# Seven inner products for P7 of the output stage, formed in place

## The chip, the cores and the metric

The kernel runs on one core of a Trainium2 chip. The metric is the device time of one execution in microseconds. Before the change it is 910.41 us, the median of three runs (909.86 to 911.19).

## What is computed

One layer of a streaming encoder on 4096 rows of 1024 channels: an RMS norm, a pooling mixer, a residual addition, a final RMS norm. With depth 1 only the pooling mixer runs:

```
def pool_mixer(h, in_w, group_w, group_b, scale, out_w):
    u, gate = jnp.split(h @ in_w, 2, axis=-1)
    ug = u.reshape(b, s, POOL_GROUPS, POOL_GROUP_DIM)
    pooled = jnp.stack([trailing_mean(ug[:, :, g], w) for g, w in enumerate(POOL_WINDOWS)],
                       axis=2) - ug
    mixed = jnp.einsum('bsgc,gcd->bsgd', pooled, group_w) + group_b
    y = mixed.reshape(b, s, POOL_WIDTH) * scale * jax.nn.silu(gate)
    return y @ out_w

h = h + pool_mixer(rms_norm(h, norm_w[0]), ...)
return rms_norm(h, final_norm_w)
```

## The kernel before

Matrices are float32. Each operand of a product is split into a high and a low part (`split`: ACT copies the high part in a shorter format, DVE subtracts it from the operand), and a product takes three passes: high by high, high by low, low by high. The three large products are done by a Strassen scheme of seven products P1 to P7 instead of eight. Stages "a" and "b" make the mixer's two halves in four blocks of 1024 rows and store y to DRAM (`yd`). The stage "o", which the change concerns, multiplies y by the output weights, adds x and applies the final norm, in eight blocks of 512 rows. In the code the blocks count from 0, so that blocks 3 to 8 of the text are b = 2 to 7 (`b > 1`).

In an output block the products run in the order P1, P7, P6, P2, P5, P4, P3. A product covers two banks of PSUM (j = 0, 1), each with four slices of the inner dimension times three passes: 24 matmuls of 128 x 512. `split_o` forms the left operand (for P7 the difference of two quarters of y) and splits it into one of four operand buffers `ops`, taken in turn by `next_op`. `evict_o` moves banks out: P1 is copied by ACT into the banks of "y" as a seed for P6, P5 and P3; P7, P6 and P2 are copied by ACT into the row tiles `hs`, to which GpSimd's accumulating DMAs add x (`add_h`); P5, P4 and P3 are added to the row tiles by DVE. After P4 the upper 256 rows of a block are complete, after P3 the lower ones, and `finish` handles them: ACT squares the two row tiles with a running sum into a junk tile, `inverse` takes the root on ACT, a reciprocal on DVE and five small steps on GpSimd, then DVE scales the two tiles and SP stores them to `out`. The last block loads x into its row tiles beforehand and ends in smaller pieces.

P2 of blocks 3 to 8 is done by a second, inner scheme of seven products (`split_inner`, `product_inner`, `add_inner`). Each inner product is 2 slices x 3 passes = 6 matmuls of 128 x 256. The inner left operand takes two of the operand buffers: the plain quarters and the four sums. The inner weights P1, P2, P3 are quarters of the weights of P2 that lie there split anyway; the four others are formed during block 2 (`load_inner`, `form_inner`) and kept, split, in four tiles.

Working tiles come from two pools: `st` (11 tiles of 128 x 1024) and `vt` (8 tiles). `take` gives the tile that has been free longest, `give` returns it; a tile whose rows are being stored is given back at once, and its next user waits for the store. Loads and splits run ahead of the products by a number of steps, `load_reach` and `split_reach`. The program is recorded in this order and then ordered for each engine by a scheduler, which `tc.issue_after` and `tc.high_priority` steer.

Of the kernel before, what the change touches and what calls it, by code (L numbers as in the profile page):

```python
# [64 lines left out]
def kernel(  # L65
# [55 lines left out]
    def renew(t):  # L121
        i = next(i for i, u in enumerate(sts) if u is t)
        return mem.tile([P, D], F32R, tag=f"st{i}", name=f"inner{i}")
# [514 lines left out]
    def load_inner():  # L638
        inner_w["raw"] = [take() for _ in range(2)]
        for h, u in enumerate(inner_w["raw"]):  # L640
            nc.sync.dma_start(out=u, in_=wod[P2][h])

    def form_inner(stage):

        pattern, sizes = "p (n k s a) -> p n k s a", dict(n=2, k=2, s=2)
        if stage == 0:
            us = inner_w.pop("raw")
            b11, b12 = (quarter(us[0], j) for j in range(2))
            b21, b22 = (quarter(us[1], j) for j in range(2))
            raw = inner_w["sums"] = [take(pattern, **sizes) for _ in range(2)]  # L650
            (t3, t2), (t1, t4) = ([r[:, n] for n in range(2)] for r in raw)
            sub(t3, b22, b12)
            add(t2, t3, b11)
            sub(t1, b22, t2)
            sub(t4, b21, t2)
            for u in us:
                give(u)
            return
        r = inner_w["sums"][stage - 1]
        hi, lo = (kept.pop().rearrange(pattern, **sizes) for _ in range(2))  # L660
        copy(hi, r)
        sub(lo, r, hi.bitcast(F32))
        give(r)
        for n, i in enumerate(((P7, P6), (P5, P4))[stage - 1]):
            inner_w[i] = [v[:, n] for v in (hi, lo)]
        for i, (h, j) in {P1: (0, 0), P2: (1, 0), P3: (1, 1)}.items():
            inner_w[i] = [quarter(w[P2][h][:, s], j) for s in range(2)]

    def split_inner(u):
# [8 lines left out]
        ts = [  # L678
            next_op("p (s g k j c) -> p s g j k c", s=2, g=2, k=2, j=2),
            next_op("p (s n k c) -> p s n k c", s=2, n=4, k=2),  # L680
        ]
        split(ts[0].rearrange("p s g j k c -> p s (g k) (j c)"), u)
        split(ts[1], v)
        give(v)
        t = {P1: ts[0][:, :, 0, 0], P2: ts[0][:, :, 1, 0], P4: ts[0][:, :, 1, 1]}
        t.update({i: ts[1][:, :, n] for n, i in enumerate((P7, P6, P5, P3))})
        return t

    def product_inner(i):

        t, sets = inner["t"], inner["sets"]
# [4 lines left out]
        for k in range(2):  # L696
            a = [t[i][:, s, k] for s in range(2)]
            b = [inner_w[i][s][:, k].rearrange("p s a -> p a s") for s in range(2)]
            ps = bank.rearrange("p (a s) -> p a s", s=2)[:, half * P : (half + 1) * P]
            for n, (x1, x2) in enumerate(((a[0], b[0]), (a[0], b[1]), (a[1], b[0]))):  # L700
                latest[0] = nc.tensor.matmul(  # L701
                    ps, x1, x2, start=i in (P1, P7) and k + n == 0, stop=k == 1 and n == 2,
                    skip_group_check=True,
                ).ins
# [11 lines left out]
    def product_out(i, t, sets, last):  # L716
# [6 lines left out]
        for j in range(2):  # L723
            if j == 1 and inner and i == P5:
# [165 lines left out]
    def load_o(b, i):  # L890
# [7 lines left out]
        elif i == P2:  # L898
            s["12"] = load_y(b, 0, 1)
            load_h(b, 1)  # L900
        elif i == P5:
# [586 lines left out]
```

## Time and profile before

| | us |
|---|---|
| median of 3 runs | 910.41 |
| profiled execution, its own time | 910.49 |
| its span, first to last instruction | 908.7 |
| TensorE busy | 900.7 |
| DVE busy | 715.5 |
| ACT busy | 485.9 |
| GpSimd busy | 84.6 |

How it is read: TensorE is PE in the profile, and PEld its loads of weights, which overlap the matmuls. A block of the output stage from block 3 on takes 35.77 us. The group lines give an engine's line and operation with out<-in, the count, the busy time, the mean ns of one, and the idle time of the engine ahead of them with what ended it. L603 is a matmul of a plain product, L701 one of an inner product, L159 and L156 a subtraction and an addition on DVE, L165 a copy on ACT, L943 a square, L947 the last scaling, L1067 an eviction by addition, L884 the DMAs that add x.

### The profile page before, as it was taken

The page shows a single profiled execution, that of the slowest core. Times are in us where ns is not written, and L with a number is a line of the kernel's source. Part 1 is how long each engine was busy: PE and PEld are TensorE (multiplying, and loading weights), DVE is VectorE, ACT ScalarE, POOL GpSimd, SP SyncE. Part 2 cuts the span into 40 slices and gives each one's busy share as a digit, 9 for nine tenths or more (in the row PEclk, how much of TensorE's full clock was granted, in tenths as well). Part 3 has the DMA queues.
Part 4 walks back from the last instruction along what each step waited for, and adds up shares of the span by engine and source line. Part 5 has one row for each costly group of instructions (what it writes and reads, how often), then busy time and mean ns, then how long its engine had stood idle before and what let it go on. Part 6 is the DMA issues. An engine that isn't in the chain of part 4 may idle for free.

```text
span 908.7 us, 11590 instructions
## 1 busy us (share of the span) xinstructions
PE 900.7 (99%) x4320; PEld 790.1 (87%) x4320; DVE 715.5 (79%) x843; ACT 485.9 (53%) x735; POOL 84.6 (9%) x166
## 2 busy tenths in 40 slices
PE   9999999999999999999999999999999999999997
PEld 7888888888888888888888888888888898988886
DVE  3889995985995997685786599599759768868686
ACT  7869547447446555355345445645545535445444
POOL 0020100100110000000000000001122113212200
PEclk9999999999999999999999999999999999999999
DMA  9987776577575454134616715618585675675732
GB/s 343 401 300 230 268 241 240 190 267 245 218 271 193 162 207 140 47 140 138 255 72 217 267 70 174 200 54 225 179 234 160 169 205 162 163 220 156 180 139 94
DMA packets 70841, 178.10 MB, mean 196 GB/s; under 512 B 6528, under 2 KB 24320, under 8 KB 70784
## 3 DMA queue, kind: packets, MB, share of 16 engines
q1 hardware_dynamic: 58160, 144.82, 46.0%
q0 software_dynamic: 11904, 31.48, 13.3%
q10 hardware_dynamic: 720, 1.06, 0.3%
q8 instruction: 34, 0.56, 0.3%
q14 instruction: 23, 0.19, 0.1%
HBM read 116.50 MB, written 60.83 MB: 195 GB/s over the span
## 4 chain that ended last, share of the span: by engine, by line
PE 95%; DVE 2%; DMA 1%; ACT 1%; issue 0%; DVEq 0%; ACTq 0%; SPq 0%
PE bank L603 89%; PE bank L701 3%; PE bank L406 3%; DMA st<-wvd 1%; DMA t3d<-st 0%; DMA early<-in_group_w 0%; DVE vt L1067 0%; DVE st L159 0%; ACT st L974 0%; ACT st L446 0%; DVE vt L162 0%; PE bank L472 0%; DVE op L159 0%; DVE vt L1026 0%; DVE st L156 0%
## 5 line engine op out<-in xcount | busy, mean ns | idle before, releaser
L603 PE MATMUL bank<-op,w 128*128 128x512 f32 x2688 | 581.2, 379 | 0.2 <-ACT st L165 0.2
L603 PEld LDWEIGHTS bank<-op,w 128*128 128x128 f32 x2688 | 507.8, 189 | 72.9 <-ACT st L165 0.6
L603 PE MATMUL bank<-w,op 128*128 128x512 f32 (+1 forms) x1212 | 262.2, 377 | 0.0
L603 PEld LDWEIGHTS bank<-w,op 128*128 128x128 f32 x1212 | 226.0, 189 | 31.0
L159 DVE TENSOR_TENSOR op<-st,op 128x1024 fp32r<-128x1024 f32 x129 | 156.5, 1220 | 76.4 <-ACT op L165 76.0
L165 ACT ACTIVATE op<-st 128x1024 fp32r<-128x1024 f32 x129 | 134.7, 1052 | 123.3 <-PE bank L603 82.6
L165 ACT ACTIVATE vt<-bank 128x512 f32<-128x512 f32 x105 | 61.4, 593 | 44.7 <-PE bank L603 44.2
L159 DVE TENSOR_TENSOR op<-vt,op 128x1024 fp32r<-128x1024 f32 x43 | 52.4, 1220 | 20.8 <-ACT op L165 20.6
L165 ACT ACTIVATE op<-vt 128x1024 fp32r<-128x1024 f32 x43 | 45.0, 1052 | 28.9 <-PE bank L603 24.9
L165 ACT ACTIVATE st<-bank 128x512 f32<-128x512 f32 x67 | 39.0, 592 | 38.0 <-PE bank L603 26.1
L884 POOL DMA_DIRECT2D st<-in_x x19 | 16.9, 894 | 387.7 <-DVE op L159 354.1
L159 DVE TENSOR_TENSOR st<-st,st 128x1024 f32<-128x1024 f32 (+1 forms) x43 | 46.7, 1108 | 3.2 <-ACT st L943 1.3
L165 ACT ACTIVATE bank<-bank 128x512 f32<-128x512 f32 x48 | 27.9, 581 | 35.6 <-PE bank L603 35.4
L755 DVE TENSOR_TENSOR_SCAN vt<-vt,window 128x1040 f32<-128x1040 f32 x16 | 38.1, 2379 | 2.8 <-ACT vt L165 2.7
L159 DVE TENSOR_TENSOR w<-st,w 128x1024 fp32r<-128x1024 f32 x25 | 30.2, 1220 | 11.7 <-ACT w L165 11.7
L165 ACT ACTIVATE w<-st 128x1024 fp32r<-128x1024 f32 x25 | 26.0, 1052 | 16.3 <-PE bank L603 10.8
L806 DVE SCALAR_TENSOR_TENSOR st<-vt,colt,st 128x512 f32<-128x512 f32 x46 | 32.4, 746 | 1.7 <-ACT st L165 1.6
L165 ACT ACTIVATE st<-st 128x1024 f32<-128x1024 f32 x16 | 16.9, 1058 | 29.9 <-DVE st L156 29.7
L801 DVE SCALAR_TENSOR_TENSOR vt<-vt,vt 128x1024 f32<-128x1024 f32 x24 | 29.3, 1221 | 0.3
L947 DVE SCALAR_TENSOR_TENSOR vt<-vt,ors,st 128x1024 f32<-128x1024 f32 x18 | 22.5, 1282 | 8.0 <-POOL ors L225 8.0
L162 DVE TENSOR_TENSOR st<-st,vt 128x1024 f32<-128x1024 f32 x22 | 26.1, 1216 | 2.1 <-DMA vt<-rd 2.1
L1067 DVE TENSOR_TENSOR st<-bank,st 128x512 f32<-128x512 f32 x23 | 15.8, 689 | 13.8 <-PE bank L603 13.7
(136 smaller groups left out, 661.6 us busy)
## 6 DMA issues: line engine op xcount, KB each, us to landing
st<-in_xt SPq DMA_DIRECT2D x28, 512.0 KB, 5.9
sd<-st POOLq DMA_DIRECT2D x28, 512.0 KB, 4.3
st<-sd SPq DMA_DIRECT2D x24, 512.0 KB, 4.4
yd<-st SPq DMA_DIRECT2D x23, 512.0 KB, 2.6
st<-in_x SPq DMA_DIRECT2D x20, 512.0 KB, 6.3
st<-yd SPq DMA_DIRECT2D x20, 512.0 KB, 4.7
out<-vt SPq DMA_DIRECT2D x18, 512.0 KB, 4.5
st<-wod SPq DMA_DIRECT2D x15, 512.0 KB, 3.4
```

Of the source, the lines that this page charges most:

```text
L159: return nc.vector.tensor_tensor(out=dst, in0=a, in1=b, op=ALU.subtract)
L162: nc.vector.tensor_tensor(out=dst, in0=a, in1=b, op=ALU.mult)
L165: return nc.scalar.activation(dst, src, func)
L406: latest[0] = nc.tensor.matmul(ps, a[:, kk, 2 * j + t, :], maps, start=t + m == 0, stop=t == 1 and m == len(pairs) - 1,).ins
L603: latest[0] = nc.tensor.matmul(ps, a, b, start=start and n == 0, stop=stop and n == 2, skip_group_check=True).ins
L701: latest[0] = nc.tensor.matmul(ps, x1, x2, start=i in (P1, P7) and k + n == 0, stop=k == 1 and n == 2, skip_group_check=True,).ins
L755: nc.vector.tensor_tensor_scan(out=sums_[:, HIST:], data0=flat[:, HIST:], data1=flat[:, HIST - win : 2 * end - win], initial=first_sum, op ...
L801: nc.vector.scalar_tensor_tensor(out=s[:, :, at : at + H], in0=s[:, :, at : at + H], scalar=1.0 / win, in1=v[:, :, HIST:], op0=ALU.mult, o ...
L806: nc.vector.scalar_tensor_tensor(out=sg[:, j], in0=s[:, j, at : at + H], scalar=bias_c[2 * grp + j], in1=sg[:, j], op0=ALU.add, op1=ALU.mult,)
L884: nc.gpsimd.dma_start(out=hs[b][half, j][:, n], in_=x[row_of(b, half, j), n * H : (n + 1) * H], accum_op=ALU.add,)
L947: nc.vector.scalar_tensor_tensor(out=us[j], in0=us[j], scalar=rs[:, j : j + 1], in1=fw[0], op0=ALU.mult, op1=ALU.mult,)
L1067: partial["added"] = nc.vector.tensor_tensor(out=dst, in0=src, in1=dst, op=ALU.add).ins
```

## The change

P7 of blocks 3 to 8 is also done as seven inner products. Unlike P2's, they are not added to row tiles one by one. Two banks make four cells of 128 x 256 (`cell`). `clear_seven` sets two of them to zero on ACT, which writes zeros during P3 of the block before. Inner products are accumulated into the cells, and copies between cells on ACT and two additions on DVE make the sums in place (`product_seven`, parts 0 to 3). Parts 0 and 1 run between the two banks of P1, part 2 in P7's place, part 3 behind P6. P7's banks are evicted there, just before P6's. One inner product (m5) is set aside in a row tile of the block, in the last block in a fresh tile.

For this the left operand of P7 is split by `split_inner` too; its four sums go into two tiles of their own (`own_op`) instead of an operand buffer. The inner weights of P7 and P2 are formed in place in the loaded tiles and split one by one (`sum_inner`, `split_weight`, `forming`), during blocks 2 and 3. Eight tiles of `st` are kept for good instead of four, in the "o" stage of blocks 1 and 2.

`finish` no longer scales and stores; `close` does so one step later. The row tiles of a block, and the load of x into half of them, are taken at P1 and P2 instead of two or more steps ahead. P5's operand is split one step ahead instead of two.

```
+    def clear_seven(b):
+        seven["v"] = sets_of("o", b)["v"]
+        for n in (0, 3):
+            nc.scalar.activation(cell(n), eps.to_broadcast([P, 2 * P]), AF.Copy, scale=0.0)
+
+    def product_seven(part, b):
+        def into(i, n):
+            leaf(seven["t"], inner_w[P7], i, seven["v"][n // 2], n % 2)
+        if part == 0:
+            into(P5, 3)
+            into(P1, 0)
+            if b == NBO - 1:
+                seven["held"] = take()
+                seven["m5"] = seven["held"][:, 0, 0 : 2 * P]
+            else:
+                seven["m5"] = hs[b][1, 0][:, 1, 0 : 2 * P]
+            copy(seven["m5"], cell(3))
+            copy(cell(2), cell(0))
+        elif part == 1:
+            into(P6, 2)
+            into(P2, 0)
+            copy(cell(1), cell(2))
+        elif part == 2:
+            into(P7, 2)
+            into(P3, 1)
+            add(cell(3), cell(2), seven["m5"])
+            add(cell(1), cell(1), seven["m5"])
+            if b == NBO - 1:
+                give(seven.pop("held"))
+        else:
+            into(P4, 2)
...
     def run(n, between=None, behind=None, seeds=4):
         kind, b, i = steps[n]
         sets = sets_of(kind, b)
-        if kind == "o":
+        if kind == "o" and b < NBO - 1 and i in (P1, P2):
+            load_h(b, int(i == P1))
+        if kind == "o" and b > 1 and i == P1:
+            seven["t"] = split_up.pop(n + 1)
+            product_out(i, split_up.pop(n), sets, False, lambda j: product_seven(j, b))
+            evict_o(b, i, sets)
+        elif kind == "o" and b > 1 and i == P7:
+            product_seven(2, b)
+        elif kind == "o" and b > 1 and i == P6:
+            product_out(i, split_up.pop(n), sets, False)
+            product_seven(3, b)
+            evict_o(b, P7, sets)
+            evict_o(b, i, sets)
+        elif kind == "o":
+            if i == P3 and 0 < b < NBO - 1:
+                clear_seven(b + 1)
             product_out(i, split_up.pop(n), sets, n == len(steps) - 1)
             evict_o(b, i, sets)
...
     def finish(b, half):
...
-        rs = inverse(b, half, ss)
+        closing.append((b, half, us, inverse(b, half, ss)))
+
+    def close():
+        b, half, us, rs = closing.pop(0)
         for j in range(2):
             nc.vector.scalar_tensor_tensor(
                 out=us[j], in0=us[j], scalar=rs[:, j : j + 1], in1=fw[0],
...
     def split_inner(u, own=False):
...
+        if own:
+            sums_op = [t.rearrange("p x (y k c) -> p (x y) k c", y=2, k=2) for t in own_op]
+            latest_copy[0] = copy(sums_op[0], v).ins
+            latest_split[0] = sub(sums_op[1], v, sums_op[0].bitcast(F32)).ins
...
     def split_reach(kind, b, i):
-        return 2 if kind == "o" and (b, i) != (0, P1) else 1
+        return 2 if kind == "o" and (b, i) != (0, P1) and not (b > 1 and i == P5) else 1
...
+    forming = {
+        (1, P7): lambda: (load_inner(P7),),
+        (1, P6): lambda: (sum_inner(P7), split_weight(P7, P5)),
+        (1, P2): lambda: (split_weight(P7, P6), split_weight(P7, P7)),
+        (1, P5): lambda: (split_weight(P7, P4), end_weights(P7), load_inner(P2)),
+        (1, P4): lambda: (sum_inner(P2),),
+        (1, P3): lambda: (split_weight(P2, P7), split_weight(P2, P6)),
+        (2, P1): lambda: (split_weight(P2, P5), split_weight(P2, P4), end_weights(P2)),
+    }
...
-        if kind == "o" and b == 1 and len(kept) < 4 and not inner_w:
-            while len(kept) < 4 and len(st.free) > 2:
-                kept.append(st.keep())
-            if len(kept) == 4:
-                load_inner()
-        elif kept:
+        if kind == "o":
+            while len(gathered) < 8 and st.free and len(st.free) + len(vt.free) > 4:
+                gathered.append(st.keep())
+                (kept if len(gathered) not in (3, 4) else own_op).append(gathered[-1])
+        if closing:
+            close()
+        if kind == "o" and b > 0:
             keep[0] = 0
```

More of the change, by code (lines that the diff above doesn't have):

```diff
@@ L636, in quarter @@
         return u.rearrange("p k (s a) -> p k s a", s=2)[:, :, :, j * P : (j + 1) * P]
[L638 to L667, printed above, removed]
@@ new lines, in split_weight, with end_weights, split_inner @@
+    def split_weight(i, p):
+        if p == P5:
+            home = [quarter(w[i][0][:, s], 1) for s in range(2)]
+        else:
+            t = kept.pop().rearrange("p k (h s a) -> p h k s a", h=2, s=2)
+            home = [t[:, s] for s in range(2)]
+        copy(home[0], raws[i][p])
+        sub(home[1], raws[i][p], home[0].bitcast(F32))
+        inner_w[i][p] = home
+    def end_weights(i):
+        for r in raws.pop(i)["held"]:
+            give(r)
+    own_op, gathered = [], []
+    def split_inner(u, own=False):
@@ L695, in product_inner @@
         }.get(i, (sets["spare"][0], 0))
[L696 to L704, printed above, removed]
+        leaf(inner["t"], inner_w[P2], i, bank, half, i in (P1, P7))
     def add_inner(bank, *places):
@@ L723, in product_out @@
         for j in range(2):
+            if between:
+                between(j)
             if j == 1 and inner and i == P5:
@@ L911, in split_o @@
             sub(s["3"], s["11"], s["21"])
+            if b > 1:
+                t = split_inner(s["3"], True)
+                give(s.pop("3"))
+                return t
+        t = next_op("p (s a b) -> p s a b", s=2, a=4)
+        if i == P7:
+            pass
         elif i == P6:
```

71 lines of the change are left out of this document (52 added, 19 removed).

## The prediction

> **What bounds the kernel now.** I read the page's header and busy times first, then who waited for whom on TensorE, then the chain that ended last in the output stage.
>
> ```profile
> span 908.7 us, 11590 instructions
> ...
> PE 900.7 (99%) x4320; PEld 790.1 (87%) x4320; DVE 715.5 (79%) x843; ACT 485.9 (53%) x735; POOL 84.6 (9%) x166
> ```
> ```profile
> PE bank L406 <- DMA early<-in_group_w: 0.4, 1, 0.4
> PE bank L603 <- ACT st L165: 0.2, 1, 0.2
> ```
> ```profile
> 712.80 25.90 PE bank L603 x120
> 738.70 3.35 PE bank L701 x30
> 742.05 2.59 PE bank L603 x12
> 744.64 0.67 PE bank L701 x6
> 745.31 2.59 PE bank L603 x12
> 747.90 0.67 PE bank L701 x6
> 748.57 25.90 PE bank L603 x120
> ```
>
> TensorE is busy for 99% of the span and never waits in the output stage: matmul follows matmul. So whatever shortens TensorE's list shortens the kernel, and every wait put into that list lengthens it one for one. The rows give two prices: 25.90/120 = 0.2158 us for a matmul of 512 columns, and 3.35/30 = 0.1117 us for one of 256. The second is more than half of the first.
>
> The other engines have time to spare on average. These are DVE, then ACT, in block 5's stretch, and TensorE in the last one (columns: stretch, its length, busy time, clock, DMA share, GB/s).
>
> ```profile
> 774.47:810.24 35.77, 25.57 (x34) 1.00 0.67 189
> ```
> ```profile
> 774.47:810.24 35.77, 17.56 (x27) 1.00 0.67 189
> ```
> ```profile
> 881.78:908.70 26.92, 20.32 (x126) 0.98 0.21 79
> ```
>
> TensorE's last matmul ends at 881.78 + 20.32 = 902.1, so 6.6 us of span lie behind it, and 910.49 - 908.7 = 1.8 us around the span.
>
> **What the change takes off TensorE.** P7 of blocks 3 to 8 was 24 matmuls of 512 columns, 24 x 0.2158 = 5.18 us. It becomes 7 x 6 = 42 of 256, 42 x 0.1117 = 4.69 us. That saves 0.49 us a block, 2.93 us in all. Were nothing late, the profiled 910.49 would become 907.56.
>
> **What it puts on the other engines.** The rows of block 5 give the prices: first DVE's, then ACT's.
>
> ```profile
> 787.91 1.21 DVE L159 TENSOR_TENSOR vt<-st,vt 128x1024 f32<-128x1024 f32 x1
> 789.05 0.42 DVE L159 TENSOR_TENSOR st<-st 128x256 f32<-128x256 f32 x1
> 789.50 0.42 DVE L159 TENSOR_TENSOR st<-st,st 128x256 f32<-128x256 f32 x1
> 789.84 0.68 DVE L1067 TENSOR_TENSOR st<-bank,st 128x512 f32<-128x512 f32 x1
> 790.48 1.23 DVE L159 TENSOR_TENSOR op<-vt,op 128x1024 fp32r<-128x1024 f32 x1
> ...
> 792.29 0.16 DVE L210 RECIPROCAL ors<-otmp 128x2 f32<-128x2 f32 x1
> 792.37 0.67 DVE L1067 TENSOR_TENSOR vt<-bank,vt 128x512 f32<-128x512 f32 x1
> 793.67 2.48 DVE L947 SCALAR_TENSOR_TENSOR st<-st,ors,st 128x1024 f32<-128x1024 f32 x2 [0.63 <-POOL ors L225]
> ```
> ```profile
> 783.49 1.06 ACT L165 ACTIVATE op<-st 128x1024 fp32r<-128x1024 f32 x1 [5.36 <-PE bank L603]
> 784.46 1.04 ACT L165 ACTIVATE op<-vt 128x1024 fp32r<-128x1024 f32 x1
> ...
> 798.11 1.06 ACT L943 ACTIVATE st<-vt 128x1024 f32<-128x1024 f32 x1 [2.54 <-DMA out<-st]
> 799.08 0.19 ACT L943 ACTIVATION_READ_ACCUMULATOR st<-vt 128x1 f32 x1
> 799.17 0.58 ACT L165 ACTIVATE bank<-bank 128x512 f32<-128x512 f32 x1
> ...
> 801.70 0.28 ACT L206 ACTIVATE otmp<-oss,eps 128x2 f32<-128x2 f32 x1
> ```
>
> From start to start in a full queue, a DVE operation on 1024 elements costs 1.13 us (1.22 to whoever waits for its result), an eviction of 512 costs 0.60 to 0.64, one of 256 costs 0.34 (0.45 if the next needs it), the two scalings 2.40. From reciprocal to scaling through POOL is 793.67 - 792.29 = 1.38. ACT's copy costs 0.97 (1.06 to its reader), a square 1.06 (1.25 with its sum read), a bank's copy 0.52 to 0.58. The row at 798.11 matters most: ACT waited there for a tile whose rows were still being stored. The scaling began at 793.67, its first half took 1.28, so that store held the tile for 798.11 - 794.95 = 3.1 us. The other prices:
>
> ```profile
> L974 ACT ACTIVATE st<-vt 128x256 f32<-128x256 f32 x2 | 0.8, 409 | 0.0
> ```
> ```profile
> out<-vt SPq DMA_DIRECT2D x16, 512.0 KB, 4.6
> st<-yd SPq DMA_DIRECT2D x10, 512.0 KB, 4.8
> ...
> out<-st SPq DMA_DIRECT2D x5, 512.0 KB, 3.4
> ```
>
> A block gains on DVE four sums of 256 (4 x 0.42), the second split of P7 (1.22) and two additions in the banks (2 x 0.42): 3.7 us. On ACT it gains the copy of that split (1.06) and five pieces of 256 (two clearings, three copies between banks; at most 5 x 0.41 by the row above): 3.1 us. DVE goes from 25.6 to about 29.3 of 35.28 us, ACT to 20.7. Neither is full, so their sums cost nothing. Once, around block 3, P7's inner weights are formed too: two loads, four sums and four splits of 512. I charge them nothing themselves: they stand in queues ahead of a stretch in which both engines wait for TensorE. Without that cover they would cost some 8 x 0.6 us of DVE.
>
> What is not covered is order. The new products need results of each other's banks: first sums, a copy out and one back, the next products, another copy, an addition. The splits for P7 and P6 stand in DVE's and ACT's queues behind the evictions, squares and scalings of the block before. Eight tiles instead of four are kept for inner weights and P7's own operands, so two buffers of one pool and eight of the other serve everything else, and a tile just given out to a store is taken again at once. In the built order of the changed kernel I followed each wait on TensorE back to the last TensorE event before it, and set the work on that path against the matmuls that cover it. Where the path is longer, TensorE stands still by the difference.
>
> **Block 3, first inner product of P7.** From the end of P4's second bank (block 2) to this product TensorE has 46 matmuls, 9.93 us. The path: eviction 0.69, square 1.25, the junk tile comes free and P2's half of y is loaded into it (4.8), ACT's copy 1.06, DVE's remainder 1.13, P7's difference 1.22, ACT's copy 1.06, and 0.2 for hand-overs: 11.4. Late by 1.4.
>
> **P6 behind it:** remainder 1.13, a sum 0.34, P6's difference 1.22, copy 1.06, against 2.45 us of matmuls: another 1.3. **Then the addition into P7's bank:** two copies of 512, two squares, another copy (4.8 with ACT's first), remainder 0.6, POOL 1.38, two scalings 2.40, P5's remainder 1.13, addition 0.42 = 10.7, against 9.2: 1.5. Behind these, three waits of 0.1 to 0.3 on the eviction and on P2's sums. Block 3: 4.8 us. Bounds 3.4 to 6.5: the load at 4 or 6, and the store that P2's sums wait for at 3.1 or 4.6.
>
> **Block 4:** P7's copied sums come 12.9 us behind P4's first eviction in a DVE queue that is full all the way, against 12.1: 0.8. The copy between banks stands behind two squares and P6's copy on ACT, 3.9 against 2.9: 1.0. Together 1.8 (0 to 2.8).
>
> **Blocks 5 to 7,** one order for all three: 0.2 at the copied sums (9.5 against 9.3), 0.5 at P6's seed, which is behind two squares and a copy on ACT (3.6 against 3.1), 0.5 at P5's remainder, which DVE reaches last. 1.2 each (0 to 2), 3.6 in all.
>
> **Block 8.** The order is another again, and stores stand in it. P7's difference takes a tile whose rows have just been scaled: eviction to scaling 5.0, store 3.1, difference 1.22, copy 1.06 make 10.4 against 9.9: 0.5. P6 follows 0.9 late, a copy 0.1. Then the worst: the last block has no row tile for the product that P7 sets aside (line "held"), and takes a fresh one, a row tile of block 7. Its path starts when P7's sums are split: square 1.25, root 0.28, POOL 1.38, scaling 1.28, store 3.1, copy out 0.41, copy to the next bank 0.41, hand-overs 0.2: 8.3, against 3.5 us of matmuls less 0.3 that the sums are early. Late by 4.5. P2's sums wait for the second store, 1.2 behind the first, then four sums of 256 and a copy (2.7), less the 0.8 of the two copies, against 1.3 of matmuls: 1.9 more. Block 8: 8.0. Bounds 4.5 (a store of 2.0, the earlier ones hidden) to 10 (a store of 4.6).
>
> This is where the deferred scaling costs: the tiles come back later than before, and P7's difference, P7's product set aside and P2's sums are the next to take them. Behind the store on SP only loads of block 8's rows wait, for evictions that come later.
>
> ```profile
> DVE vt L947 <- POOL ors L225: 7.0, 8, 1.2
> ```
>
> What the deferral was worth to DVE is in the paths already: before, DVE stood 0.6 to 1.2 us between reciprocal and scaling for POOL; now the next eviction and a sum or two stand between them, and 0.1 to 0.5 is left. The reciprocal and POOL's five steps stay where they were; two scalings move behind one product's evictions on DVE, two stores behind a load of y on SP.
>
> **The rest.** Row tiles taken later: the halves for P3 are loaded at P2 instead of earlier, and their reader is three products, 15 us, away against a landing of 4.8: nothing. P7's rows are evicted with P6, one product later, so their accumulating DMAs have only some 6 us until P5's eviction.
>
> ```profile
> DMA to landing us min/median/max: 4.1/6.0/8.8
> ```
>
> At the median that is just enough, at 8.8 it is 2 us late: 0 here, up to 2 in the range. The tail behind the last matmul: as before, 6.6.
>
> **Clock.** Early matmuls of 256 are slower than later ones (columns: busy, mean ns):
>
> ```profile
> L406 PE MATMUL bank<-early,early 128*128 128x256 f32 x96 | 22.3, 390 | 0.4 <-DMA early<-in_group_w 0.4
> ...
> L406 PE MATMUL bank<-w,w 128*128 128x256 f32 x48 | 5.7, 279 | 0.0
> ```
>
> [...]
>
> **Sum.** 910.49 - 2.93 + 4.8 + 1.8 + 3.6 + 8.0 = 925.8. The profiled execution is 0.1 us above the median of the runs shown, so 925.7. Low end of the waits 3.4 + 0 + 0 + 4.5 = 7.9 gives 915.4; high end 6.5 + 2.8 + 6 + 10 = 25.3 gives 932.8.
>
> **Rivals.**
> - Nothing late: 907.5, faster. Mechanism: DVE and ACT run far enough ahead. In block 5 ACT waited 5.36 us for TensorE at 783.49; were the new splits all fed from such reserves, every path above would be covered. It decides from the point at which all waits together stay below 2.93 us. Against it: two paths begin at an eviction and one at a split, which no reserve moves, and three hold a transfer. Chance 11%.
> - Only the stores bind: blocks 3 and 8 as above, DVE's queues never late in blocks 4 to 7: 925.7 - 5.4 = 920.3. For it: 0.2 to 0.5 us late is within what a queue of 30 operations may be off by. Chance 25%.
> - Accumulating DMAs late: P5's eviction waits 2 us more in blocks 3 to 6, of which none is hidden since DVE's queue is full behind it: 925.7 + 8 = 933.7. For it: landings up to 8.8. Against: half land under 6.0. Chance 9%.
> - No change within measurement: the waits happen to equal the gain. 4%.
>
> The forecast of 925.7 keeps 51%. The range must hold the forecast and the second rival: 914 to 933. About 0.2% (1.8 us) is what this kernel's runs can tell from no change. Chances: faster 0.11, same 0.04, slower 0.85.
>
> **What would show it.** Right: TensorE waits in the output stage where there were none, the longest (4 to 5 us) in block 8 on an ACT copy between banks, with ACT's wait for a store of rows just ahead; a wait of more than 1 us for ACT's copy of P7's difference in block 3; blocks 5 to 7 of 36.0 to 37 us instead of 35.77. Wrong: blocks of 35.3 us and TensorE as full as before, which would mean that my paths are too long throughout; or block 8's wait gone, if the set-aside tile is free earlier than the built order says.

## The result and the profile after

The changed kernel takes 935.27 us (median of 4, 934.5 to 935.68), against 910.28 of the kernel before beside it: 1.027 times as long (1.0257 to 1.029). It is slower, as predicted, and by more: 25 us instead of 15, 2 us beyond the end of the range.

The page of the changed kernel, header and busy times:

```profile
span 933.9 us, 11905 instructions
...
PE 908.6 (97%) x4428; PEld 793.5 (85%) x4428; DVE 739.9 (79%) x895; ACT 500.2 (54%) x777; POOL 84.3 (9%) x166
```

TensorE has 108 more matmuls, as the change says (6 x (42 - 24)). It fell from 99% to 97% of a span that grew by 25 us. Who waited for whom on TensorE, the list that was all but empty for the output stage before:

```profile
PE bank L711 <- ACT op L165: 4.9, 4, 2.0
PE bank L711 <- ACT bank L165: 4.9, 2, 4.2
PE bank L711 <- ACT inner L165: 3.0, 4, 0.7
PE bank L603 <- ACT op L165: 1.9, 2, 1.4
...
PE bank L711 <- DVE bank L156: 0.8, 1, 0.8
PE bank L603 <- DVE op L159: 0.6, 3, 0.2
```

In this kernel L603 is a plain matmul, L711 one of an inner product (L701 before), L165 any copy on ACT, L159 a subtraction on DVE. The waits are where the prediction put them: ACT's copies of operands and copies between banks. The listed 16 us are less than what was lost. TensorE's timeline for blocks 3, 6 and 8 shows it (columns: start, length, what, count, idle before and its releaser):

```profile
693.51 0.49 PE L711 MATMUL bank<-w,op 128*128 128x256 f32 x2 [2.00 <-ACT op L165]
...
697.71 1.13 PE L603 MATMUL bank<-w,op 128*128 128x512 f32 x4 [1.40 <-ACT op L165]
...
708.61 0.94 PE L711 MATMUL bank<-inner,op 128*128 128x256 f32 x6 [0.75 <-DVE bank L156]
...
713.79 0.49 PE L711 MATMUL bank<-w,op 128*128 128x256 f32 x2 [1.48 <-ACT op L165]
...
805.93 3.62 PE L603 MATMUL bank<-w,op 128*128 128x512 f32 x16
810.29 0.49 PE L711 MATMUL bank<-w,inner 128*128 128x256 f32 x2 [0.74 <-ACT inner L165]
810.62 1.89 PE L603 MATMUL bank<-w,op 128*128 128x512 f32 x8
...
813.80 1.56 PE L603 MATMUL bank<-w,op 128*128 128x512 f32 x6
815.20 0.83 PE L711 MATMUL bank<-inner,inner 128*128 128x256 f32 x6
...
826.27 2.43 PE L603 MATMUL bank<-w,op 128*128 128x512 f32 x10 [0.22 <-DVE op L159]
...
899.86 0.94 PE L711 MATMUL bank<-inner,inner 128*128 128x256 f32 x6 [4.20 <-ACT bank L165]
...
903.13 0.80 PE L711 MATMUL bank<-w,op 128*128 128x256 f32 x2 [1.17 <-ACT op L165]
...
903.93 1.49 PE L711 MATMUL bank<-inner,inner 128*128 128x256 f32 x6
905.22 1.49 PE L711 MATMUL bank<-w,inner 128*128 128x256 f32 x6
```

Take 805.93: 16 matmuls at 0.2158 end at 809.38, the next start at 810.29. That is 0.91 lost, where the row lists 0.74: by its length of 3.62 the group before it ends at 809.55, 0.17 later than by 16 x 0.2158. Behind a wait, the first two matmuls of 256 take 0.33 from start to start (810.29 to 810.62) instead of 0.22: another 0.1. And at 813.80 no wait is listed at all, yet 813.15 + 4 x 0.1117 = 813.60, so 0.20 is lost, and 0.1 behind it (813.80 + 6 x 0.2158 = 815.09, next 815.20). Added up in this way, start against start, over all groups of TensorE:

| block | 3 | 4 | 5 | 6 | 7 | 8 | sum |
|---|---|---|---|---|---|---|---|
| predicted | 4.8 | 1.8 | 1.2 | 1.2 | 1.2 | 8.0 | 18.2 |
| measured | 8.1 | 2.6 | 2.1 | 2.1 | 2.1 | 10.7 | 27.6 |

The tail behind the last matmul grew as well: 916.84 + 9.32 = 926.16 is its end, 7.7 us ahead of the span's, against 6.6. 910.49 - 2.93 + 27.6 + 1.1 = 936.3; the execution took 935.65, and the 0.6 between lie ahead of the output stage: that stage's first matmul starts at 614.71 us in the kernel before and at 614.08 in the changed one.

The longest wait, 4.20 us in block 8, is the one that the prediction named. ACT's copy of the set-aside product stands at a store of rows, and DVE's first sum for P2 at the store behind it:

```profile
899.02 0.38 ACT L165 ACTIVATE vt<-bank 128x256 f32<-128x256 f32 x1 [2.48 <-DMA out<-vt]
...
900.32 0.42 DVE L159 TENSOR_TENSOR vt<-vt 128x256 f32<-128x256 f32 x1 [0.81 <-DMA out<-vt]
```

Block 8's loss is not waits alone. The clock granted to TensorE there (columns: stretch, length, busy time, clock, DMA share, GB/s):

```profile
899.86:901.40 1.54, 1.54 (x11) 0.81 0.00 0
901.40:907.60 6.20, 5.03 (x24) 0.50 0.01 3
907.60:912.00 4.40, 4.35 (x25) 1.00 0.00 0
```

Behind the wait of 4.20 us the clock falls to half. In the timeline above six matmuls of 256 take 1.29 us (903.93 to 905.22) instead of 0.67; up to 908.9 this costs some 2.3 us. The prediction's sum has no term for it.

### The profile page after: what moved, and what is told of

The parts are those of the page before. It is cut to its first block, busy times and chain, and to the rows that moved or that the text cites. A ratio compares the mean times of both kernels' runs of the same rounds, so it can differ in the third digit from the quotient of the medians.

```text
span 933.9 us, 11905 instructions
## 1 busy us (share of the span) xinstructions
PE 908.6 (97%) x4428; PEld 793.5 (85%) x4428; DVE 739.9 (79%) x895; ACT 500.2 (54%) x777; POOL 84.3 (9%) x166
## 3 DMA queue, kind: packets, MB, share of 16 engines
q10 hardware_dynamic: 720, 1.06, 0.3%
## 4 chain that ended last, share of the span: by engine, by line
PE 78%; DVE 10%; ACT 4%; DMA 4%; issue 3%; POOL 1%; DVEq 0%; POOLq 0%; ACTq 0%
PE bank L603 73%; PE bank L406 3%; DVE op L159 3%; PE bank L711 2%; DVE vt L159 2%; DVE vt L1021 2%; ACT op L165 2%; DVE vt L1141 1%; DMA out<-vt 1%; DMA vt<-wod 1%; ACT vt L1014 1%; DVE st L156 1%; DVE inner L159 0%; ACT vt L165 0%; DMA vt<-yd 0%
## 5 line engine op out<-in xcount | busy, mean ns | idle before, releaser
L603 PE MATMUL bank<-op,w 128*128 128x512 f32 x2688 | 580.9, 379 | 0.0
L603 PEld LDWEIGHTS bank<-op,w 128*128 128x128 f32 x2688 | 507.8, 189 | 72.4 <-ACT bank L165 0.4
L603 PE MATMUL bank<-w,op 128*128 128x512 f32 (+1 forms) x1068 | 238.2, 378 | 2.9 <-ACT op L165 1.9
L603 PEld LDWEIGHTS bank<-w,op 128*128 128x128 f32 x1068 | 196.1, 189 | 31.6 <-ACT op L165 2.8
L159 DVE TENSOR_TENSOR op<-st,op 128x1024 fp32r<-128x1024 f32 x106 | 128.8, 1220 | 71.7 <-ACT op L165 71.3
L165 ACT ACTIVATE op<-st 128x1024 fp32r<-128x1024 f32 x106 | 110.7, 1051 | 73.7 <-PE bank L603 50.1
L165 ACT ACTIVATE op<-vt 128x1024 fp32r<-128x1024 f32 x66 | 69.4, 1055 | 76.3 <-PE bank L603 26.2
L165 ACT ACTIVATE vt<-bank 128x512 f32<-128x512 f32 (+1 forms) x126 | 71.3, 583 | 54.7 <-PE bank L603 43.5
L159 DVE TENSOR_TENSOR op<-vt,op 128x1024 fp32r<-128x1024 f32 x66 | 80.4, 1220 | 22.9 <-ACT op L165 22.6
L946 POOL DMA_DIRECT2D vt<-in_x x38 | 33.6, 923 | 440.4 <-DVE vt L817 354.2
L165 ACT ACTIVATE bank<-bank 128x512 f32<-128x512 f32 (+1 forms) x60 | 31.8, 536 | 40.0 <-PE bank L603 33.3
L1141 DVE TENSOR_TENSOR vt<-bank,vt 128x512 f32<-128x512 f32 (+1 forms) x51 | 34.2, 675 | 16.2 <-PE bank L603 15.5
L165 ACT ACTIVATE st<-bank 128x512 f32<-128x512 f32 x52 | 30.2, 594 | 30.4 <-PE bank L603 19.1
L159 DVE TENSOR_TENSOR w<-st,w 128x1024 fp32r<-128x1024 f32 x25 | 30.2, 1219 | 11.7 <-ACT w L165 11.6
L1014 ACT ACTIVATE vt<-vt 128x1024 f32<-128x1024 f32 x25 | 26.2, 1049 | 24.1 <-DVE vt L1141 23.7
L159 DVE TENSOR_TENSOR st<-st,st 128x1024 f32<-128x1024 f32 x32 | 38.1, 1217 | 1.3 <-ACT st L246 0.6
L711 PE MATMUL bank<-w,op 128*128 128x256 f32 x216 | 31.6, 282 | 4.9 <-ACT op L165 4.9
L711 PEld LDWEIGHTS bank<-w,op 128*128 128x128 f32 x216 | 29.0, 195 | 7.5 <-ACT op L165 6.5
L165 ACT ACTIVATE w<-st 128x1024 fp32r<-128x1024 f32 x25 | 26.0, 1051 | 16.8 <-PE bank L603 12.2
```

The lines of the kernel that those rows point to most:

```text
L159: return nc.vector.tensor_tensor(out=dst, in0=a, in1=b, op=ALU.subtract)
L165: return nc.scalar.activation(dst, src, func)
L603: latest[0] = nc.tensor.matmul(ps, a, b, start=start and n == 0, stop=stop and n == 2, skip_group_check=True).ins
L711: latest[0] = nc.tensor.matmul(ps, x1, x2, start=start and k + n == 0, stop=k == 1 and n == 2, skip_group_check=True,).ins
L946: nc.gpsimd.dma_start(out=hs[b][half, j][:, n], in_=x[row_of(b, half, j), n * H : (n + 1) * H], accum_op=ALU.add,)
L1014: nc.scalar.activation(junk, us[j], AF.Square, accum_out=ss[:, j : j + 1])
```

## The experiments

Each changes one thing in the changed kernel unless it says otherwise. The last columns add up TensorE's losses by block as above; "others" is the mean of blocks 4 to 7. These sums are of the one profiled execution of each run, which lies up to 1.9 us from the median (no_sums_quarter_squares: 921.04 against 919.10).

| run | us | ratio to before | block 3 | others | block 8 |
|---|---|---|---|---|---|
| the changed kernel | 935.27 | 1.0257 to 1.029 | 8.1 | 2.2 | 10.7 |
| plain_p7_all | 916.28 | 1.0055 to 1.0085 | 3.5 | 0 | 1.9 |
| plain_p7_one_set | 912.10 | 1.001 to 1.003 | 0 | 0 | 2.0 |
| plain_p7_block8 | 926.47 | 1.017 to 1.0204 | 7.3 | 2.2 | 1.8 |
| own_rows_block8 | 929.39 | 1.0195 to 1.0226 | 7.1 | 2.2 | 3.6 |
| scaling_at_once | 934.28 | 1.0254 to 1.0284 | 6.6 | 2.2 | 10.4 |
| p2_weights_later | 935.24 | 1.0254 to 1.0293 | 9.0 | 2.0 | 9.6 |
| one_set_of_weights | 928.99 | 1.0192 to 1.0226 | 2.1 | 2.1 | 10.9 |
| no_p7_sums | 929.93 | 1.0193 to 1.0239 | 7.2 | 2.2 | 6.2 |
| quarter_squares | 929.09 | 1.019 to 1.0234 | 8.9 | 1.6 | 6.2 |
| no_sums_quarter_squares | 919.10 | 1.0086 to 1.0116 | 4.1 | 0.2 | 8.0 |
| p7_sums_first | 933.10 | 1.0239 to 1.027 | 9.0 | 1.9 | 8.4 |
| all_three | 921.18 | 1.0116 to 1.0146 | 1.8 | 1.8 | 3.7 |

Block 3 lost 8.1, 7.3 and 7.1 in three kernels whose order up to there is the same, so a single figure of it is good to 1 us. In p2_weights_later, quarter_squares and p7_sums_first block 3 also holds a stretch of some 3.4 us at half clock (0.50 from 712.05 to 715.47 in the first and from 715.00 to 718.40 in the third; in quarter_squares the pace of the matmuls shows it, five of 256 in 1.06 us from 712.32 instead of 0.56), which the other runs do not have there; it is 1.5 to 1.7 us of the 9 that each of them loses.

### What the rest of the change costs without the seven products

plain_p7_all: P7 plain in every block, all else kept (the plain weights of P7 have one quarter overwritten by an inner weight).

```
-            if b > 1:
+            if b > NBO:
                 t = split_inner(s["3"], True)
...
-        if kind == "o" and b > 1 and i == P1:
+        if kind == "o" and b > NBO and i == P1:
...
```

> P7 of every block is two plain products again, so TensorE's list is that of the kernel before (910.3 us). All else of the change stays: eight tiles kept, P7's inner weights loaded and formed though unused, the scaling a product later, the row tiles taken later. Theory A (the seven products bring the waits, by their own sums, copies and additions): no waits are left, 909.5 to 911.5. Theory B (the tiles kept for them and the forming of the weights bring a part of the waits by themselves: in block 3 the load of P2's inner weights, which took 10.43 us, stands ahead of evictions on DVE, and in block 8 the operand of P7 and the sums of P2 still take tiles that are being stored): about 3.5 us of waits in block 3, 2.7 in block 8, none between: 916.5 (915 to 918).

Measured 916.28, theory B. TensorE's timeline, blocks 3 and 8:

```profile
693.64 1.13 PE L603 MATMUL bank<-w,op 128*128 128x512 f32 x4 [1.24 <-ACT op L165]
...
702.50 4.58 PE L603 MATMUL bank<-w,op 128*128 128x512 f32 x20 [0.99 <-DVE op L159]
...
888.33 0.71 PE L711 MATMUL bank<-w,op 128*128 128x256 f32 x4 [0.72 <-ACT op L165]
```

The waits in block 3 are for P7's and P6's operands, those in block 8 for P2's sums. So some 6 us are lost to the rest of the change, with P7 plain throughout. plain_p7_one_set then leaves out the forming of P7's weights (P2 of block 2 reads plain weights of which one quarter is already overwritten):

```
-        (1, P7): lambda: (load_inner(P7),),
+        (1, P7): lambda: (load_inner(P2),),
...
-        (1, P5): lambda: (split_weight(P7, P4), end_weights(P7), load_inner(P2)),
+        (1, P5): lambda: (split_weight(P2, P4), end_weights(P2), inner_w.update({P7: inner_w[P2]})),
-        (1, P4): lambda: (sum_inner(P2),),
...
```

> P7 is two plain products in every block, and only one set of inner weights is formed, where the change puts P7's (one quarter of P2's plain weights is overwritten as in the kernels before and after); eight tiles are kept, the scaling stays a product later. What is left of the change is the scarcity of tiles and the moved scaling. Theory A (of the 6.2 us that plain products still lost, 3.5 were the second forming): no wait in block 3, some 2.3 us in block 8 (P7's operand and P2's sums behind a store), 911.5 to 913.5. Theory B (scarce tiles alone make block 3 late): 914.5 or more.

Measured 912.10, theory A. In the output stage two listed waits are left, both in block 8:

```profile
PE bank L711 <- ACT op L165: 0.7, 1, 0.7
...
PE bank L603 <- DVE op L159: 0.2, 1, 0.2
```

The second forming costs 4.2 us here, the scarce tiles and the moved scaling 2, and those in block 8 alone.

### Block 8

plain_p7_block8: P7 plain in the last block only (one quarter of its weights is overwritten here too).

```
-        if kind == "o" and b > 1 and i == P1:
+        if kind == "o" and 1 < b < NBO - 1 and i == P1:
...
```

> Only the last block's P7 is two plain products again. The trace of the changed kernel puts block 8 some 10.8 us behind its matmuls, the half-speed matmuls behind the longest wait among them. Theory A (all of that is due to the seven products in this block): 935.3 - 10.8 + 0.5 = 925.0 (924 to 926). Theory B (part of it is due to scarce tiles, which stay scarce): the operand of P7 and the sums of P2 still wait for a store, some 2.7 us in all: 927.7 (926.5 to 929). If lateness were only carried over from blocks 3 to 7, on DVE and ACT, block 8 would keep most of it: above 930.

926.47, between A and B: the seven products cost block 8 8.9 us (10.7 - 1.8), and 1.8 stay, for the reason that plain_p7_one_set showed. So nothing is carried over into block 8 from blocks 3 to 7, which lose here what they lost. own_rows_block8 keeps the products and moves the one set aside:

```
-                seven["held"] = take()
-                seven["m5"] = seven["held"][:, 0, 0 : 2 * P]
+                seven["m5"] = hs[b][1, 0][:, 1, 0 : 2 * P]
...
-                give(seven.pop("held"))
+                nc.sync.dma_start(out=hs[b][1, 0][:, 1], in_=x[row_of(b, 1, 0), H:])
...
```

> In block 8 the product that P7 sets aside goes into the block's own rows, as in the other blocks, and that half of x is loaded behind the addition; no fresh tile is taken. Theory A (the wait of 4.20 us is for the store of the rows whose tile is taken, and the half-speed matmuls behind it, 2.2 us, come from that wait): both are gone, 935.3 - 4.4 - 2.2 = 928.7; P2's sums then take the tile of the first of the two stores, up to 1.2 us earlier, so 926 to 929. Theory B (P2's sums come when they came, behind the second store, and TensorE stands still there in place of here): 933 to 935. Theory C (the half speed has nothing to do with the wait): 930.9, with the granted clock still near 0.66 just behind P7's additions.

929.39, 0.4 above theory A's range, and by its mechanism: the long wait is gone and so is the half clock, which theory C would have kept. TensorE's timeline at this place:

```profile
888.56 1.13 PE L603 MATMUL bank<-w,op 128*128 128x512 f32 x4 [0.55 <-ACT op L165]
...
899.48 3.37 PE L603 MATMUL bank<-w,op 128*128 128x512 f32 x14 [1.12 <-DVE vt L1139]
```

The clock over the stretch:

```profile
897.00:907.00 10.00, 8.88 (x50) 1.00 0.26 95
```

A wait of 1.12 us for an eviction into a row tile takes its place; block 8 falls from 10.7 to 3.6. So the store that the fresh tile waits for cost the wait of 4.4 us and, through the clock, 2.3 more, half as much again.

### The moved scaling

```
         closing.append((b, half, us, inverse(b, half, ss)))
+        close()
```

> The last scaling and the store of the rows follow their reciprocal at once again, in every block. Theory A (the deferral costs, as the prediction has it: tiles come back one eviction and a sum or two later, 0.7 us or more at each of two places in a block, and P7's difference, the product set aside and P2's sums wait for those tiles): 2 to 4 us of the loss come back, 931 to 933. Theory B (between reciprocal and scaling DVE waits for POOL anyway, 1.38 us, and the next eviction fits into that; the stores come hardly earlier): 934 to 935.5.

934.28, theory B: 1.0 us less, and the intervals overlap. Blocks 4 to 7 lose exactly what they lost. The deferral as such costs next to nothing.

### The weights of blocks 2 and 3

In the changed kernel the chain of waits holds two transfers around block 3 (columns: start, length, what):

```profile
668.21 10.43 DMA vt<-wod
...
705.91 4.96 DMA out<-vt
```

DVE's timeline shows who stood at them; its rows from 799.65 on are of block 6, and the last row is ACT's:

```profile
678.73 0.69 DVE L159 TENSOR_TENSOR vt<-vt,vt 128x512 f32<-128x512 f32 x1 [4.77 <-DMA vt<-wod]
...
710.97 0.42 DVE L159 TENSOR_TENSOR vt<-vt 128x256 f32<-128x256 f32 x1 [2.08 <-DMA out<-vt]
...
799.65 1.23 DVE L159 TENSOR_TENSOR vt<-vt,st 128x1024 f32<-128x1024 f32 x1 [1.26 <-ACT vt L1014]
...
803.74 0.40 DVE L159 TENSOR_TENSOR vt<-vt 128x256 f32<-128x256 f32 x1
...
805.06 2.48 DVE L1021 SCALAR_TENSOR_TENSOR vt<-vt,ors,st 128x1024 f32<-128x1024 f32 x2 [0.32 <-POOL ors L225]
807.46 0.42 DVE L159 TENSOR_TENSOR vt<-vt,vt 128x256 f32<-128x256 f32 x1
...
808.73 0.42 DVE L159 TENSOR_TENSOR vt<-vt,vt 128x256 f32<-128x256 f32 x1
...
809.18 1.06 ACT L165 ACTIVATE inner<-vt 128x1024 fp32r<-128x1024 f32 x1 [2.86 <-DVE vt L159]
```

The load of P2's inner weights took 10.43 us. DVE reached their first sum at 673.96 and stood 4.77 us, with P4's evictions behind it. p2_weights_later moves the sums and the splits:

```
-        (1, P4): lambda: (sum_inner(P2),),
-        (1, P3): lambda: (split_weight(P2, P7), split_weight(P2, P6)),
-        (2, P1): lambda: (split_weight(P2, P5), split_weight(P2, P4), end_weights(P2)),
+        (1, P3): lambda: (sum_inner(P2),),
+        (2, P7): lambda: (split_weight(P2, P7), split_weight(P2, P6)),
+        (2, P6): lambda: (split_weight(P2, P5), split_weight(P2, P4), end_weights(P2)),
```

> The sums of P2's inner weights are taken a product later (their loads start where they did), and the four splits behind them as well. Theory A (block 3 is later than predicted, 7.3 against 4.8 us, because DVE stands 4.77 us at the load of these weights, which took 10.43, with P4's evictions behind it): DVE no longer waits there, the squares, the load of y and P7's operand come earlier, and block 3 falls back by 1.5 to 3 us: 932 to 934. Theory B (the weights' sums and splits cost their time wherever they stand, since they only move behind the operands of P7 and P6): the wait at P7's first product gets shorter but others take its place: 934.5 to 936.5.

935.24, theory B: the wait at P7's first product shrank from 2.00 to 0.42, and the one for P2's operand grew from 1.48 to 2.74, behind a store at which DVE now stood 3.22. TensorE's timeline:

```profile
693.08 0.49 PE L711 MATMUL bank<-w,op 128*128 128x256 f32 x2 [0.42 <-ACT op L165]
...
712.52 0.79 PE L711 MATMUL bank<-w,op 128*128 128x256 f32 x2 [2.74 <-ACT op L165]
```

DVE's, at the first of P2's sums:

```profile
709.70 0.43 DVE L159 TENSOR_TENSOR vt<-vt 128x256 f32<-128x256 f32 x1 [3.22 <-DMA out<-vt]
```

During this wait the clock falls to half (columns as for block 8):

```profile
712.05:715.47 3.42, 2.95 (x9) 0.50 1.05 198
```

That is 1.5 us of the 9.0 which block 3 loses in this run. Without it block 3 would lose 7.5, against 7.1 to 8.1 in the three kernels named above, so theory A, by which 1.5 to 3 us should have come back, falls even so: a product later, the forming only moves the waits. one_set_of_weights takes the work away, by the same edit as in plain_p7_one_set, with the seven products left in (P7's products use P2's inner weights, and P2 of block 2 reads a quarter already overwritten).

> Only one set of inner weights is loaded and formed, P2's, at the place where the change puts P7's; the seven products of P7 multiply with them too (so P7's rows are wrong). Products, sums, copies and tiles are those of the changed kernel; gone are two loads, four sums and eight pieces of splits behind P5 of block 2. Theory A (the second forming is what makes blocks 3 and 4 later than the steady ones, 7.3 and 2.7 us against 2.1): both fall to some 2.1, 935.3 - 5.8 = 929.5 (928.5 to 931.5). Theory B (the seven products cost more in block 3 by themselves, because half the tiles are new and the first path begins at block 2's end): block 3 keeps 4 us or more, 932 to 934.

928.99, theory A: blocks 3 and 4 lose 2.1 each, as every other. TensorE's waits:

```profile
PE bank L711 <- ACT bank L165: 4.5, 1, 4.5
PE bank L711 <- ACT inner L165: 3.7, 5, 0.7
```

Five equal waits for P7's copied sums, one a block, and the one of block 8. The second forming costs 6.3 us, nearly all of it in block 3 (8.1 to 2.1).

### The steady 2.1 us of a block

DVE's rows of block 6 above give the path. P7's difference (799.65) waits 1.26 us for ACT's square, because it takes the tile into which the square was written. From there DVE is all but full; both scalings (805.06) stand between the first sum of P7 (803.74) and the second (807.46). The last sum is done at 809.15 (808.73), ACT's copy of the four takes until 810.24 (809.18), and TensorE goes on at 810.29. This is a reading of the rows; two runs take work from one queue each. no_p7_sums:

```
         sub(v[:, 0], a11, a21)
-        sub(v[:, 1], a22, v[:, 0])
-        add(v[:, 2], v[:, 1], a11)
-        sub(v[:, 3], a12, v[:, 1])
+        if not own:
...
```

> Three of the four sums of 256 that P7's operand needs are left out in every block from 3 on, and the other split is taken from the difference itself (P7's values are wrong then); TensorE, ACT, the tiles and the transfers do what they did. DVE has 3 x 0.34 = 1.0 us less to do between the evictions of one block and P6's operand. Theory A (blocks 4 to 7 are late, 2.1 to 2.7 us each, because DVE's queue is full from P4's first eviction on and everything for P7 and P6 comes out of it): the wait of 0.74 for P7's copied sums and the wait for P5's remainder go, a block falls from 37.35 to 36.0 to 36.6, and with block 8's shorter path the whole to 922 to 928. Theory B (ACT's queue sets these waits, by two squares and three copies between banks): blocks stay above 37.0 and the whole above 932.

quarter_squares:

```
-            nc.scalar.activation(junk, us[j], AF.Square, accum_out=ss[:, j : j + 1])
+            nc.scalar.activation(junk[:, :, 0 : H // 4], us[j][:, :, 0 : H // 4], AF.Square, accum_out=ss[:, j : j + 1])
```

> The squares of blocks 1 to 7 read a quarter of each row (so the rows' scale is wrong); ACT has some 2 x 0.65 us less to do at the end of each half block, DVE what it had. Theory A (DVE's queue alone): blocks 5 to 7 stay at 37.0 or more, the whole at 930 or more, since only the paths that begin with a square are shorter. Theory B (ACT's queue): blocks at 36.3 or less, the whole below 926. Both queues in turn: 36.5 to 37.0, 926 to 931.

929.93 and 929.09, but most of both comes from block 8: in both runs its wait for the set-aside product is 1.8 us instead of 4.4, and the matmuls behind it keep their full pace (the first six of 256 take 0.77 and 0.78 us, 0.67 and a restart of 0.1). The steady blocks hardly moved, from 2.1 to 2.0 (and 2.7 in block 7), and from 2.1 to 1.6: theory A of the first fell (and the whole is not above theory B's 932 either, because of block 8), and the second came out at 36.88 us a block, both queues in turn. TensorE's longest lists of waits, first of no_p7_sums (L713 is there the matmul of an inner product), then of quarter_squares:

```profile
PE bank L713 <- ACT bank L165: 8.2, 7, 1.9
```
```profile
PE bank L711 <- ACT inner L165: 3.9, 5, 0.9
```

With less work on DVE the copies between banks are what TensorE waits for, with less work on ACT it is P7's copied sums as before. So both together, no_sums_quarter_squares:

> Both at once: three of P7's four sums left out, and the squares of a quarter of each row (values are wrong in P7's rows and in the rows' scale). DVE has 1.0 us less to do at the turn of a block, ACT some 1.3. Singly they brought blocks 5 to 7 from 37.35 to 37.24 and 36.88 us. Theory A (the two queues are in turn the longer one; taking from one only shows the other): the waits go and blocks come near their matmuls, 35.3 to 35.9, the whole 916 to 922. Theory B (the gains add singly, as there is a third cause, such as the order of the products themselves): 36.7 or more, the whole 924 to 928.

919.10, theory A. TensorE in three stretches of a steady block's length, with both edits:

```profile
727.00:762.00 35.00, 35.00 (x204) 1.00 0.65 181
762.00:797.00 35.00, 35.00 (x204) 1.00 0.66 181
797.00:832.00 35.00, 35.00 (x205) 1.00 0.66 180
```

And one such stretch of the changed kernel:

```profile
762.00:797.00 35.00, 34.01 (x195) 1.00 0.62 172
```

35.00 of 35.00 us, with the seven products in place and all their copies between banks. The steady loss lies in what DVE and ACT do at the turn of a block, and taking work from one alone leaves the other's. How much of it is work and how much is order stays open: the edits also shorten the paths, and they let the scheduler order DVE's list anew (in quarter_squares P6's sum stands ahead of an eviction, 799.54 and 800.68, in the changed kernel behind it, 801.40 and 800.80). What this run still loses is block 3's forming and, in block 8, a wait of 2.68 us for P6's remainder with half clock behind it. p7_sums_first only changes the order:

```
-                t = split_inner(s["3"], True)
+                with tc.high_priority():
+                    t = split_inner(s["3"], True)
```

> P7's four sums and their split get a higher priority, so that DVE does them behind P7's difference, ahead of the last scaling and the evictions that stand between the first and the second sum in the changed kernel; the work is the same. Theory A (it is the place in DVE's queue: the scaling, 2.40 us, and two evictions, 1.2, are ahead of three of the sums): the wait of 0.74 us at P7's copied sums goes and little takes its place, blocks of 36.3 to 36.8 us instead of 37.35, the whole 930 to 933. Theory B (the queue is full, what is put ahead makes the rest late by as much): the wait moves to P6's operand and seed or to P5's remainder, blocks of 37.1 us and more, the whole above 934.

933.10. Blocks 6 and 7 came to 37.09 (the wait for copied sums stays at 0.71, the one for P5's remainder is no longer listed), closer to theory B: this order of the same work gives back 0.26 us there (block 4 gains 1.3, block 5 loses 0.4 more). The 2.2 us of the whole come mostly from block 8 (10.7 to 8.4), where the half clock lasts 3.4 us and not 6.8.

### All three repairs

> One set of inner weights (P7's rows are wrong), P7's sums first, and block 8's product set aside in its own rows, together. If the three losses are separate: the gains of the single runs add, 935.3 less some 5.5, 4 and 6: 919 to 922, still 9 to 12 us above the kernel before, as waits of about 1.3 us a block stay. If they overlap (a block that is less late at its start waits more at its next place): 923 or more.

The edits of one_set_of_weights, p7_sums_first and own_rows_block8. 921.18: the single runs gave 6.3 + 2.2 + 5.9 = 14.4, together they give 14.1. That these totals agree is partly luck, as the 2.2 come mostly from block 8, which own_rows_block8 mends as well. By blocks the losses are separate: one set of weights takes 6.6 us from blocks 3 and 4, the own rows 7.0 from block 8, the order 0.26 from each of five blocks, 14.9 in all, and the sum over the blocks falls by 14.9, from 27.6 to 12.7. A kernel that beats the one before was not found: even with only one set of weights formed, where the scheme needs two, 1.8 us a block stay against a gain of 0.49.

## Why the prediction was right in kind and short by some 10 us

Of the 9.4 us by which the waits came out above the forecast, 3.3 lie in block 3, 0.8 in block 4, 2.7 in blocks 5 to 7 and 2.7 in block 8.

- **The gain, 0.49 a block.** Holds: no_sums_quarter_squares runs the same matmuls with TensorE full.
- **Block 8, wait for the set-aside product, 4.5:** 4.4. **Wait for P2's sums, 1.9:** 1.8. **P7's difference, P6 and a copy, 1.5:** 1.8. The mechanism and its sizes hold; own_rows_block8 shows it for the first, the longest.
- **The clock, in no term of the sum:** the step that failed in block 8; measured 2.3 us. The trace before could not show it: the clock granted there is 1.00 from 6.60 to 902.10 us, the end of the matmuls. The early matmuls that the prediction gives under "Clock" hardly show a slow one: four of the 96 start in the first 6.35 us, over 1.57 us, and the other 92 are mostly 0.22 us apart, as matmuls of 512 columns are.
- **P7's inner weights: "I charge them nothing themselves":** the step that failed in block 3. The runs put 6.3 us on the second forming (4.2 with plain products). Pieces of it may be in the prediction's paths for block 3, which make 4.8 and not 1.2 as in a steady block, but it names none. Start against start, P7's first product was 2.2 late (1.4 predicted), P6 1.6 (1.3), the addition 0.9 (1.5) and P2's operand 1.6, against "0.1 to 0.3"; 0.1 for each restart makes up most of the rest. P2's sums stood behind a store of 4.96, where the prediction took 3.1 to 4.6. The load of these weights, 10.43 us, is in none of its paths (its "load at 4 or 6" is of y, which held the chain for 3.86); that this load alone is the cause is refuted by p2_weights_later, and which piece of the forming costs how much was not separated.
- **Blocks 5 to 7, 1.2 each:** the step that failed there; measured 2.1, or 37.35 us a block, above the 36.0 to 37 that the prediction gave as a sign of being right. The three waits are those named, but the copied sums are 0.9 late and not 0.2 (DVE stands 1.26 us for the square's tile in that path; but in quarter_squares it stands 0.62 and the sums are 1.0 late, so this wait alone is not the cause), P6's seed 0.2, P5's remainder 0.4, and each of the waits, even one of 0.04 (ahead of 812.61), costs 0.1 more to start again (there four matmuls of 256 take 0.54 and not 0.45). That restart was in no term. With it falls "Neither is full, so their sums cost nothing": in block 6 DVE was busy for 29.98 of 37.35 us and ACT for 19.45, and yet three sums less on DVE and shorter squares on ACT brought the 2.1 back.
- **"This is where the deferred scaling costs":** wrong as said. Undone alone, it gives back 1.0 us. What costs is that a tile is being stored when it is taken. That this comes from keeping eight tiles is argued, since the deferral alone was ruled out; no run keeps fewer.
- **The tail, as before:** it grew by 1.1, and in every run with seven products in block 8 it is 7.1 us or more (6.6 to 7.0 where P7 is plain there). Why was not followed further.
- **The rivals.** Stores alone do not bind: blocks 5 to 7 lose 2.1 without one. The accumulating DMAs were not late in the changed kernel: DVE's list of waits there has no entry for them. The upper end of the range was made from the bounds of paths and left out restarts, clock and tail, 0.1 x some 30 + 2.3 + 1.1 = some 6 us. Some of its sums are off by up to 0.1 us (798.11 - 794.95 is 3.2, 11.4 - 9.93 is 1.5), which moves the total by no more than that.

## What to carry to other kernels

Where one engine is full and sets the end, price a change not by the work that it adds to the others but by the order in which their results are due, and add a fixed cost for every wait it creates; here that was 0.1 us each, and half as much again for the one of 4 us, because of the clock. Preparations done once (here a second set of weights) run in the same queues and tiles, so they belong in the sum. And two engines that take turns in being late hide each other: taking work from one brought 0.1 and 0.5 us of the 2.1 of a steady block, from both all of it.

## What the runs showed of the hardware

The half clock came here in stretches of some 3.4 and 6.8 us. In the changed kernel it is 6.20 us at 0.50 and (1 - 0.81) / 0.5 x 1.54 = 0.6 ahead of it, 6.8 in all; in no_sums_quarter_squares it is 6.80 us at 0.50 (881.60 to 888.40), from within the wait of 2.68 on. In p7_sums_first a stretch of 3.4 us appears in block 3 as well, behind a wait of only 1.67 us (1.84 by start against start):

```profile
713.42 0.49 PE L711 MATMUL bank<-w,op 128*128 128x256 f32 x2 [1.67 <-ACT op L165]
```
```profile
715.00:718.40 3.40, 3.40 (x13) 0.50 0.88 275
```

The changed kernel's wait of 1.48 us (1.64) in the same place left the clock at full speed, and so did its longer wait of 2.00 us at 693.51 in the same block (columns as for block 8):

```profile
687.00:721.80 34.80, 29.07 (x165) 1.00 0.59 172
```

So the length of the listed wait alone does not tell whether the clock falls: it fell behind 1.67 us in p7_sums_first, and did not behind 2.00 us in the changed kernel. These runs do not show what decides it.

The 0.1 us lost to a restart behind a wait (0.33 instead of 0.22 at 810.29) is no property of small matmuls: no_sums_quarter_squares has the same groups back to back without it, six of 256 in 0.67 us (730.67 to 731.34).
